# Layer 1's attention in chunks of 1024 keys instead of 512, with PSUM buffers of two banks

## The chip, the cores and the metric

The kernel runs on one core of a Trainium2 chip. A core has five engines with an instruction queue each: TensorE (PE in the profile; its weight loads are listed apart, as PEld), VectorE (DVE), ScalarE (ACT), GpSimd (POOL) and SyncE (SP), which here only issues DMAs. TensorE writes its results into PSUM, 8 banks of 512 fp32 values per partition; DVE and ACT read them there. Everything else lies in SBUF or in DRAM. The metric is the time of one execution on the device in microseconds (us).

## The reference

A trunk of two layers on x of shape 1 x 2048 x 1024, in fp32. Layer 0 (two kinds of windowed attention) is not touched. Layer 1 projects the normalized stream to q, k, v and a gate, and runs differential attention with 8 heads: each head has two score maps over the same keys, and the second is taken off the first with a learned factor. Queries see all keys of their own chunk of 64 and of the chunks before it.

```python
def block(i):                       # 128 queries
    mask = (kchunk[None, :] <= qchunk[:, None])[None, None]
    s1 = jnp.einsum('bqhd,bkhd->bhqk', qb1, k1) * scale
    s2 = jnp.einsum('bqhd,bkhd->bhqk', qb2, k2) * scale
    p1 = jax.nn.softmax(jnp.where(mask, s1, NEG_INF), axis=-1)
    p2 = jax.nn.softmax(jnp.where(mask, s2, NEG_INF), axis=-1)
    a = p1 - lam * p2
    return jnp.einsum('bhqk,bkhd->bqhd', a, v)    # v has 128 columns a head
```

The result of each head goes through an RMS norm, is multiplied with silu(gate), and all heads go through an output projection that is added to the stream.

## The kernel before

Layer 1 runs in two steps: `project` writes q, k, v and the normalized hidden stream to DRAM, and `_mix1` does the rest. The change lies in `_mix1`. There the 2048 queries are 4 blocks of 512 (b = 0 to 3), each of 4 rows of 128 queries (j). A pair of head and block is the unit of work; `heads` runs them as (h, 0), (h, 1) for each of the 8 heads, then block 2 for all heads, then block 3.

**Scores (`scores`, L927 on).** A row with nk visible keys is cut into chunks of up to 512 keys. For each of the two maps (m) and each chunk (z), PE does two matmuls (L949 and L950: the query in a high and a low part, packed against the keys' parts) into one PSUM bank from the pool `pS`, which has `BANKS1[0]` = 4 of them. DVE writes a large negative value over the corner that the last chunk must mask (L952), takes the negated maximum of the chunk (L953), and ACT reads the bank once more and writes exp(score - maximum) into an SBUF tile, with the sum of the row in an accumulator (L956; the read of that accumulator is an ACT record of its own). That exponential is the last reader of the bank. The tiles of the first map come from the pool `pp` (20 tiles of 512), those of the second from `sb` under the tag P1 (8 tiles).

**Joining the chunks (L962 to L976).** Each chunk has its own maximum, so rows of several chunks need factors: the smallest negated maximum, differences, an exponential of them, and sums, on tiny tiles. Rows of one chunk skip this.

**Combining (`combine`, L981 on).** One row later, for each chunk: ACT scales the second map's tile by its factor and lambda (L987), POOL scales the first map's tile (L988) and adds the two (L989). The combined probabilities stay in the first map's tile. `combine` is queued behind the first exponential of the next row.

**Values (`values`).** For each tile of 128 keys, PE transposes the probabilities of up to four rows into a PSUM bank (L1001; pool `ptr`, 2 banks), DVE copies them to SBUF (L1003), and PE multiplies them with v into an accumulator of one bank (L1005; pool `pO`). Then `gate` normalizes and gates the head's output on ACT, DVE and POOL (L1023 to L1037), with one matmul for the mean square (L1033).

**Side work.** `gates` (L1095 on) makes the gate projection, 8 x 8 steps of three matmuls a block (L214 to L216), and `projected` the output projection of finished blocks, in the same form, in the one bank of `pG`; the last block's projection (`projected_last`) runs at the end, when `pS` is free, and keeps its output tiles there.

**Order.** `pace` writes the order: it takes steps of `heads` (each yields a chunk's keys / 256) and of the queue of `values` (each yields its columns / 128) so that the scores lead by `LAG1` (30 or 36) units, and takes side steps in proportion to the units done, by `STAGES1`. This is the order in the code only: the program is built with `schedule_with_timeline_sim=True`, with which the compiler lists the instructions of each engine by a timeline of its own, in the order of the code where operands and buffers are ready. A gate or output step may not come ahead of the score matmul last traced before it (`self.anchor`, `issue_after`). SP issues all loads: q of the next head at row 2, keys and values by `then`, called after each chunk.

## Time and profile before

| | us |
|---|---|
| three runs | 2795.34, 2809.33, 2809.50; median 2809.33 |
| the profiled execution | 2806.47 |
| its span, first to last instruction | 2804.3 |
| first score matmul of layer 1 (L949) starts | 1732.7 |
| last score matmul of layer 1 (L950) starts | 2720.7 |
| 512-key score matmuls of 1 part (L949), in number | 448 |
| score chunks in all (exponentials at L956), in number | 640 |

All rows of the profile come from the one profiled execution; the other runs have a total time only. A row of a group reads: line, engine, operation, written tile <- read tiles, shapes, count | busy time, mean ns of one | idle time of the engine just before them, and what ended it. A row of the waits reads: who waited <- for whom: us in total, times, longest. A row of the timeline reads: start, duration, engine, line, operation. A row of the windows reads: from:to, length, then busy time and number of instructions of each engine, the clock granted to PE as a share of full speed, and DMA. The durations of matmuls are those of a pipelined engine: each overlaps the next, so that their distance from start to start, not their duration, is what they cost.

### The profile page before, as it was taken

Reading aid. Unit: us, or ns where it says so; the run is one execution under the profiler, and the core shown is the slowest. Engines: PE = TensorE matmul, PEld = TensorE weight load, DVE = VectorE, ACT = ScalarE, POOL = GpSimd, SP = SyncE. Lnnn points to the kernel's source line nnn. Section 1 sums busy time; section 2 is a strip of 40 time slices with the busy share of each in tenths; the row PEclk is TensorE's granted clock in tenths of the full one; section 3 lists DMA queues with packets and bytes.
Section 4 is the critical chain, followed back from the end, with each engine's and each line's share of the span. In section 5 each row is a group of like instructions: output and inputs, shape, how many; then the busy total and the mean of one; then the engine's idle time right before and its main releaser. Section 6 shows DMA issues by size and latency. Waiting matters only on the chain.

```text
span 2804.3 us, 43657 instructions
## 1 busy us (share of the span) xinstructions
PE 2691.3 (96%) x13384; PEld 2166.5 (77%) x13384; DVE 1822.1 (65%) x4520; ACT 1599.4 (57%) x3975; POOL 1431.7 (51%) x1519
## 2 busy tenths in 40 slices
PE   7999999999899999999999999999999999999998
PEld 6888887888788888788888888767676777676776
DVE  7752285336777776457834783478886887777762
ACT  5443544357767775333343332578886777776661
POOL 3641254245545454336453652367675666767671
PEclk9999999999999999999999999999999999999999
DMA  5673348739877774754495347788867676464542
GB/s 177 226 240 139 109 148 271 239 111 248 223 196 192 191 196 144 238 190 128 143 297 187 124 134 211 219 232 225 215 194 223 178 210 200 124 190 134 162 154 80
DMA packets 354041, 521.64 MB, mean 186 GB/s; under 512 B 42768, under 2 KB 137744, under 8 KB 353808
## 3 DMA queue, kind: packets, MB, share of 16 engines
q1 hardware_dynamic: 349200, 510.47, 60.6%
q10 hardware_dynamic: 4608, 8.39, 0.8%
q8 instruction: 107, 1.75, 0.3%
q14 instruction: 126, 1.03, 0.1%
HBM read 361.70 MB, written 157.02 MB: 185 GB/s over the span
## 4 chain that ended last, share of the span: by engine, by line
PE 69%; DMA 7%; DVE 3%; ACT 2%; issue 1%; POOL 1%; SPq 0%; ACTq 0%; DVEq 0%; POOLq 0%
PE cO L1005 8%; PE p1mm L216 6%; PE p1mm L215 6%; PE p1mm L214 6%; PE cS L949 4%; PE cS L950 4%; PE ctr L1001 4%; PE com L214 2%; PE com L215 2%; PE com L216 2%; PE mom L214 2%; PE mom L215 2%; PE mom L216 2%; PE mtrB L775 2%; PE cG L214 2%; PE cG L216 2%
## 5 line engine op out<-in xcount | busy, mean ns | idle before, releaser
L956 ACT ACTIVATE cP<-cS,cnm 128x512 f32<-128x512 f32 (+3 forms) x640 | 394.3, 621 | 145.2 <-DVE cnm L953 134.2
L953 DVE TENSOR_REDUCE cnm<-cS 128x1 f32<-128x512 f32 (+3 forms) x640 | 374.7, 602 | 61.5 <-PE cS L950 55.0
L989 POOL TENSOR_TENSOR cP<-cP,cP 128x512 f32<-128x512 f32 (+1 forms) x320 | 358.3, 1148 | 43.7 <-ACT cP L987 43.1
L988 POOL TENSOR_SCALAR cP<-cP,crl,cel 128x512 f32<-128x512 f32 (+3 forms) x288 | 209.9, 743 | 237.9 <-DVE crl L970 136.1
L214 PE MATMUL p1mm<-p1wH,p1hH 128*128 128x512 f32 x768 | 300.1, 392 | 1.2 <-ACT p1hH L334 1.2
L216 PE MATMUL p1mm<-p1wH,p1hL 128*128 128x512 f32 x768 | 300.4, 392 | 0.0
L215 PE MATMUL p1mm<-p1wL,p1hH 128*128 128x512 f32 x768 | 299.3, 390 | 0.0
L309 POOL TENSOR_TENSOR p0wL<-p0ws,p0wH 128x512 fp32r<-128x512 f32 (+1 forms) x140 | 169.9, 1241 | 247.5 <-ACT p0wH L307 228.4
L1005 PE MATMUL cO<-cpt,cv 128*128 128x512 f32 (+3 forms) x640 | 290.1, 538 | 2.9 <-DVE cpt L1003 2.8
L949 PE MATMUL cS<-ck,cqd 128*128 128x512 f32 (+3 forms) x640 | 265.2, 418 | 17.1 <-ACT cP L956 13.7
L1003 DVE COPY cpt<-ctr 128x512 f32<-128x512 f32 (+1 forms) x320 | 191.4, 605 | 112.5 <-PE ctr L1001 109.1
L214 PE MATMUL p0mm<-p0wH,p0hH 128*128 128x512 f32 (+1 forms) x640 | 237.8, 375 | 6.7 <-ACT p0vt L497 4.7
L216 PE MATMUL p0mm<-p0wH,p0hL 128*128 128x512 f32 (+1 forms) x640 | 238.8, 374 | 1.5 <-DVE p0hL L335 1.5
L950 PE MATMUL cS<-ck,cql 128*128 128x512 f32 (+3 forms) x640 | 233.7, 369 | 5.8 <-DMA cql<-qL 5.8
L215 PE MATMUL p0mm<-p0wL,p0hH 128*128 128x512 f32 (+1 forms) x640 | 238.8, 373 | 0.0
L1001 PEld LDWEIGHTS ctr<-ident,cP 128*128 128x128 f32 x1088 | 139.0, 142 | 120.4 <-issue 64.9
L309 POOL TENSOR_TENSOR p1wL<-p1ws,p1wH 128x512 fp32r<-128x512 f32 x112 | 154.4, 1402 | 137.8 <-ACT p1wH L307 126.6
L987 ACT ACTIVATE cP<-cP,cc 128x512 f32<-128x512 f32 (+1 forms) x320 | 189.1, 651 | 22.9 <-DVE cc L973 22.4
L1001 PE MATMUL ctr<-ident,cP 128*128 128x128 f32 x1088 | 177.1, 275 | 5.2 <-ACT csq L1034 3.6
L214 PEld LDWEIGHTS p1mm<-p1wH,p1hH 128*128 128x128 f32 x768 | 144.3, 188 | 29.9 <-ACT p1hH L334 1.4
L216 PEld LDWEIGHTS p1mm<-p1wH,p1hL 128*128 128x128 f32 x768 | 144.2, 188 | 29.4
L215 PEld LDWEIGHTS p1mm<-p1wL,p1hH 128*128 128x128 f32 x768 | 144.3, 188 | 29.1
(302 smaller groups left out, 6945.4 us busy)
## 6 DMA issues: line engine op xcount, KB each, us to landing
p1ws<-in_od_w_in_dram SPq DMA_DIRECT2D x56, 512.0 KB, 3.7
p0ws<-in_ev_w_in_dram SPq DMA_DIRECT2D x48, 512.0 KB, 4.6
ck<-kH SPq DMA_DIRECT2D x144, 128.0 KB, 3.6
ck<-kL SPq DMA_DIRECT2D x144, 128.0 KB, 3.8
cv<-v SPq DMA_DIRECT2D x72, 256.0 KB, 4.3
cqd<-qH SPq DMA_DIRECT2D x64, 256.0 KB, 5.9
cql<-qL SPq DMA_DIRECT2D x64, 256.0 KB, 7.8
cwH<-wgH SPq DMA_DIRECT2D x64, 256.0 KB, 5.4
```

Of the source, the lines that this page charges most:

```text
L214: mm(ps, aH, bH, start=first, stop=False)
L215: mm(ps, aH, bL, start=False, stop=False)
L216: mm(ps, aL, bH, start=False, stop=last)
L309: low.tensor_tensor(l[:, :width], ws[:, k, :width], f32(h[:, :width]), ALU.subtract)
L949: mm(ps, qd[:, m, js], kt[:, :wd], start=True, stop=False)
L950: self.anchor = mm(ps, ql[:, m, js], kt[:, :wd], start=False, stop=True).ins
L953: nc.vector.tensor_reduce(nm[:, m, z:z + 1], ps, AX.X, ALU.max, negate=True)
L956: exp = nc.scalar.activation(chunks[z][:, :wd], ps, AF.Exp, bias=nm[:, m, z:z + 1], accum_out=acc).ins
L988: nc.gpsimd.tensor_scalar(p1, p1, rl[:, 0:1], e1, ALU.mult, ALU.mult)
L989: nc.gpsimd.tensor_tensor(p1, p1, p2, ALU.add)
L1001: nc.tensor.transpose(turned[:, (j - j0) * P:(j - j0 + 1) * P], us[j][kt // 4][:, kk:kk + P], self.ident)
L1005: mm(O[:, j0 * P:], v, T[:, :wd], start=(kt == 0), stop=(kt == nkt - 1), skip_group_check=True)
```

## The change

`WIDE` = 1024. Scores are cut into chunks of up to 1024 keys. The PSUM pool `pS` has 2 buffers of two banks in place of 4 of one; PE fills such a buffer 512 keys at a time, with the same two matmuls for each 512. The mask, the maximum, the exponential, the scaling copy and POOL's two operations then run once for a chunk of up to 1024 keys. Rows of block 1 become one chunk (before: two), those of blocks 2 and 3 two (before: three and four); rows of block 0 stay one chunk of at most 512. The probability tiles become 1024 wide, half as many. In blocks 0 and 2, two chunks of at most 512 keys share such a place (`place_of`). `values` finds its columns by kt // 8 in place of kt // 4. The output projection of the last block takes halves of a two-bank buffer (`bank`), and its weights use three wide P1 places in place of six narrow ones. The number of units that a chunk yields still is its keys / 256, and the lags and stages of `pace` are as before.

```diff
--- before.py
+++ after.py
@@ -24,6 +24,7 @@
 BLK = NTB * P
 NB = S // BLK
 HD = 64
+WIDE = 2 * BLK
 EPS = 1e-6
 NEG = -1e30
 POS = -NEG
@@ -89,7 +90,7 @@
     AHEAD = ((0, 2), (0, 3), (1, 2), (1, 3)), ((0, 5), (1, 0))
     BANKS0, LAG0, SHARE0 = (3, 3, 1, 1), 9, 0.85
     FIN = 18
-    BANKS1, LAG1 = (4, 2, 1, 1), (30, 30, 36, 36)
+    BANKS1, LAG1 = (2, 2, 1, 1), (30, 30, 36, 36)
     STAGES1 = ((0, 0), (44, 84), (1088, 504))
 
     def __init__(self, ctx, tc, args, out):
@@ -895,7 +896,7 @@
         n = "c"
         pool = lambda nm, bufs, **kw: es.enter_context(tc.tile_pool(name=n + nm, bufs=bufs, **kw))
         ld = pool("ld", 2)
-        pp = pool("pp", 20)
+        pp = pool("pp", 10)
         ot = pool("ot", 4)
         vp = pool("v", 4)
         yp = pool("y", 2 * KT)
@@ -929,14 +930,26 @@
 
             qd, ql = q
             us = res["u"] = []
+            halves = [[], []]
+
+            def place_of(m, wd):
+
+                if wd <= BLK and halves[m]:
+                    return halves[m].pop()
+                pl = sb if m else pp
+                t = pl.tile([P, WIDE], F32, tag=f"P{m}", name=n + f"P{m}", bufs=4 if m else None)
+                if wd <= BLK and b % 2 == 0:
+                    halves[m].append(t[:, BLK:])
+                return t
+
             for j in range(NTB):
                 t = b * NTB + j
                 nk = (t + 1) * P
-                cuts = [(c, min(nk, c + 512)) for c in range(0, nk, 512)]
+                cuts = [(c, min(nk, c + WIDE)) for c in range(0, nk, WIDE)]
                 nb = len(cuts)
                 js = slice(j * P, (j + 1) * P)
-                nm = small("nm", 8).rearrange("p (m z) -> p m z", m=2)
-                el = small("el", 16).rearrange("p (m z i) -> p m z i", m=2, i=2)
+                nm = small("nm", 4).rearrange("p (m z) -> p m z", m=2)
+                el = small("el", 8).rearrange("p (m z i) -> p m z i", m=2, i=2)
                 e, la = el[:, :, :, 0], el[:, :, :, 1]
                 l, rl = small("l", 2), small("rl", 2)
                 rows = []
@@ -944,33 +957,36 @@
                     chunks = []
                     for z, (c, ce) in enumerate(cuts):
                         wd = ce - c
-                        ps = pS.tile([P, 512], F32, tag="S", name=n + "S")[:, :wd]
-                        kt = K[z, m]
-                        mm(ps, qd[:, m, js], kt[:, :wd], start=True, stop=False)
-                        self.anchor = mm(ps, ql[:, m, js], kt[:, :wd], start=False, stop=True).ins
+                        ps = pS.tile([P, WIDE], F32, tag="S", name=n + "S")[:, :wd]
+                        for o in range(0, wd, BLK):
+                            oe = min(wd, o + BLK)
+                            kt = K[(c + o) // BLK, m]
+                            mm(ps[:, o:oe], qd[:, m, js], kt[:, :oe - o], start=True, stop=False)
+                            self.anchor = mm(ps[:, o:oe], ql[:, m, js], kt[:, :oe - o], start=False, stop=True).ins
                         if ce == nk:
                             nc.vector.memset(ps[0:HD, wd - 64:], NEG)
                         nc.vector.tensor_reduce(nm[:, m, z:z + 1], ps, AX.X, ALU.max, negate=True)
-                        chunks.append((sb if m else pp).tile([P, 512], F32, tag=f"P{m}", name=n + f"P{m}", bufs=8 if m else None))
+                        chunks.append(place_of(m, wd))
                         acc = la[:, m, z:z + 1] if nb > 1 else l[:, m:m + 1]
                         exp = nc.scalar.activation(chunks[z][:, :wd], ps, AF.Exp, bias=nm[:, m, z:z + 1], accum_out=acc).ins
                         while parts:
                             parts.pop(0)(exp)
-                        then(j, m, z)
+                        for o in range(c, ce, BLK):
+                            then(j, m, o // BLK)
                         yield wd / 256
                     rows.append(chunks)
                 if nb > 1:
-                    top, pe = small("top", 2), small("pe", 8).rearrange("p (m z) -> p m z", m=2)[:, :, :nb]
-                    nc.vector.tensor_reduce(top, nm[:, :, :nb], AX.X, ALU.min)
-                    below = small("below", 8).rearrange("p (m z) -> p m z", m=2)[:, :, :nb]
-                    nc.vector.tensor_tensor(below, nm[:, :, :nb], top.unsqueeze(2).to_broadcast([P, 2, nb]), ALU.subtract)
-                    nc.scalar.activation(e[:, :, :nb], below, AF.Exp, scale=-1.0)
-                    nc.vector.tensor_reduce(pe, el[:, :, :nb, :], AX.X, ALU.mult)
+                    top, pe = small("top", 2), small("pe", 4).rearrange("p (m z) -> p m z", m=2)
+                    nc.vector.tensor_reduce(top, nm, AX.X, ALU.min)
+                    below = small("below", 4).rearrange("p (m z) -> p m z", m=2)
+                    nc.vector.tensor_tensor(below, nm, top.unsqueeze(2).to_broadcast([P, 2, nb]), ALU.subtract)
+                    nc.scalar.activation(e, below, AF.Exp, scale=-1.0)
+                    nc.vector.tensor_reduce(pe, el, AX.X, ALU.mult)
                     nc.vector.tensor_reduce(l, pe, AX.X, ALU.add)
                 nc.vector.reciprocal(rl, l)
-                c2 = small("c2", 4)[:, :nb]
+                c2 = small("c2", 2)[:, :nb]
                 if nb > 1:
-                    nc.vector.tensor_scalar(c2, e[:, 1, :nb], rl[:, 1:2], self.nlam, ALU.mult, ALU.mult)
+                    nc.vector.tensor_scalar(c2, e[:, 1, :], rl[:, 1:2], self.nlam, ALU.mult, ALU.mult)
                 else:
                     nc.vector.tensor_scalar(c2, rl[:, 1:2], self.nlam, None, ALU.mult)
                 parts.append(lambda exp, r=(rows, cuts, e, rl, c2): combine(exp, *r))
@@ -996,9 +1012,9 @@
                 j0 = max(0, kt - b * NTB)
                 wd = (NTB - j0) * P
                 turned = ptr.tile([P, 512], F32, tag="tr", name=n + "tr")
-                kk = (kt % 4) * P
+                kk, ku = (kt % 4) * P, (kt % 8) * P
                 for j in range(j0, NTB):
-                    nc.tensor.transpose(turned[:, (j - j0) * P:(j - j0 + 1) * P], us[j][kt // 4][:, kk:kk + P], self.ident)
+                    nc.tensor.transpose(turned[:, (j - j0) * P:(j - j0 + 1) * P], us[j][kt // 8][:, ku:ku + P], self.ident)
                 T = tp.tile([P, 512], F32, tag="pt", name=n + "pt")
                 nc.vector.tensor_copy(T[:, :wd], turned[:, :wd])
                 v = res["v"][kt // 4][:, kk:kk + P]
@@ -1119,14 +1135,22 @@
                     nc.sync.dma_start(s["g"][c * P:(c + 1) * P, tok], gt)
                     yield 1
 
-        def out_begin(b, j, c, pl=None, tag="S"):
+        banks = []
+
+        def bank(pl):
+
+            if pl is pG:
+                return pG.tile([P, 512], F32, tag="G", name=n + "om")
+            if not banks:
+                t = pS.tile([P, WIDE], F32, tag="S", name=n + "om")
+                banks.extend((t[:, BLK:], t[:, :BLK]))
+            return banks.pop()
+
+        def out_begin(b, j, c, pl=None):
             rows, cols = slice((b * NTB + j) * P, (b * NTB + j + 1) * P), slice(c * 512, (c + 1) * 512)
             xr = ot.tile([P, BLK], F32, tag="ot", name=n + "xr")
             nc.sync.dma_start(xr, self.x1[rows, cols])
-            if b < NB - 1:
-                pl, tag = pG, "G"
-            pl = pl or pS
-            return xr, pl.tile([P, 512], F32, tag=tag, name=n + "om"), self.out[rows, cols]
+            return xr, bank(pG if b < NB - 1 else pl), self.out[rows, cols]
 
         def out_step(b, j, k, ps, w):
             js = slice(j * P, (j + 1) * P)
@@ -1158,16 +1182,11 @@
 
             b = NB - 1
             w = [(room[0][:, k, :], room[1][:, k, :]) for k in range(KT)], []
-            tags = [(ld, "qd"), (ld, "ql")] * 2, [(sb, "P1")] * 6 + [(kp, "k0"), (kp, "k1")]
             pairs = []
-            for pl, tag in tags[0]:
-                t = pl.tile([P, 2, BLK], F32R, tag=tag, name=n + "w" + tag)
+            for pl, tag in [(ld, "qd"), (ld, "ql")] * 2 + [(sb, "P1")] * 3:
+                t = pl.tile([P, 2, BLK], F32R, tag=tag, name=n + "w" + tag, bufs=4 if tag == "P1" else None)
                 pairs.append((t[:, 0, :], t[:, 1, :]))
-            for i in range(4):
-                pairs.append([
-                    pl.tile([P, BLK], F32R, tag=tag, name=n + "w" + tag, bufs=8 if tag == "P1" else None)
-                    for pl, tag in tags[1][2 * i:2 * i + 2]
-                ])
+            pairs.append([kp.tile([P, BLK], F32R, tag=tag, name=n + "w" + tag) for tag in ("k0", "k1")])
             for k in range(KT):
                 load_w(0, k, pairs[k])
             def step(js, tiles, w, k):
@@ -1180,7 +1199,7 @@
             first = [out_begin(b, j, 1) for j in range(NTB)]
             for k in range(KT - 1):
                 yield from step(range(NTB), first, w[0], k)
-            ahead = [out_begin(b, 0, 0, pG, "G")]
+            ahead = [out_begin(b, 0, 0, pG)]
             for k in range(KT - 1):
                 yield from step((0,), ahead, pairs, k)
             yield from step(range(NTB), first, w[0], KT - 1)
```

## The prediction, made before the changed kernel was run

> **What bounds the kernel now.** I read the page first: what each engine does in the whole span, and who is on the chain that ended last.
>
> ```profile
> span 2804.3 us, 43657 instructions
> ...
> PE 2691.3 (96%) x13384; PEld 2166.5 (77%) x13384; DVE 1822.1 (65%) x4520; ACT 1599.4 (57%) x3975; POOL 1431.7 (51%) x1519
> ...
> PE 69%; DMA 7%; DVE 3%; ACT 2%; issue 1%; POOL 1%; SPq 0%; ACTq 0%; DVEq 0%; POOLq 0%
> ```
>
> TensorE (PE) is busy for 96% and has 69% of the chain; no other engine has more than 3%. The change touches only layer 1's attention, so I cut that stretch (it starts near 1733 us and runs to the end) into parts with the view of windows: the start, the interleaved heads of query blocks 0 and 1, block 2, block 3 and the tail. The limits come from the first starts of the score matmuls and the order in `heads`; the inner ones are round numbers that I chose.
>
> ```profile
> core 0: us, PE busy (x) PEld busy (x) DVE busy (x) ACT busy (x) POOL busy (x), PEclk, DMA share, GB/s
> 1733.00:1850.00 117.00, 105.88 (x480) 82.40 (x478) 56.17 (x194) 64.52 (x176) 48.04 (x59) 0.96 0.82 237
> 1850.00:2030.00 180.00, 170.34 (x804) 125.75 (x804) 153.61 (x472) 154.65 (x424) 127.29 (x142) 0.98 0.81 218
> 2030.00:2350.00 320.00, 313.96 (x1434) 230.62 (x1433) 255.08 (x636) 250.78 (x653) 212.96 (x227) 0.99 0.69 204
> 2350.00:2725.00 375.00, 359.23 (x1601) 259.17 (x1600) 276.34 (x623) 266.76 (x684) 259.67 (x264) 0.98 0.50 149
> 2725.00:2804.30 79.30, 70.65 (x299) 52.14 (x296) 18.58 (x29) 11.54 (x19) 16.33 (x15) 0.95 0.32 108
> sum 1071.30, PE 1020.05 PEld 750.08 DVE 759.78 ACT 748.25 POOL 664.30; mean PE 204.01 PEld 150.02 DVE 151.96 ACT 149.65 POOL 132.86
> ```
>
> In 1071 us PE is busy for 1020 and idle for 51. ACT and DVE are nowhere full: they come closest in the second part, at 154.65 and 153.61 of 180 us. So work taken from ACT and DVE is worth only what PE waits for them. That is the view of waits, PE alone, over the same stretch:
>
> ```profile
> PE cS L949 <- ACT cP L956: 13.7, 12, 6.4
> PE cG L214 <- DMA cwH<-wgH: 5.8, 3, 3.3
> PE cS L950 <- DMA cql<-qL: 5.8, 4, 3.3
> PE com L214 <- ACT cyk L1059: 3.7, 1, 3.7
> PE ctr L1001 <- ACT csq L1034: 3.6, 1, 3.6
> PE com L214 <- ACT cy L1059: 3.5, 1, 3.5
> ```
>
> The largest is 13.7 us in 12 waits: a score matmul that waits until an exponential has emptied a PSUM buffer. ACT is named in 13.7 + 3.7 + 3.6 + 3.5 = 24.5 us; the rest is mostly DMA, which the change leaves alone. **24.5 us, 0.9%, is the most that a faster ACT can give.**
>
> **The change part by part.** First the work on ACT and DVE. The view of groups by line, shapes kept apart, has a wide and a narrow form of each operation:
>
> ```profile
> L956 ACT ACTIVATE cP<-cS,cnm 128x512 f32<-128x512 f32 x448 | 305.3, 685 | 121.7 <-DVE cnm L953 112.6 <-PE ctr L1001 3.1 <-DVE cl L969 1.4
> L956 ACT ACTIVATION_READ_ACCUMULATOR cP<-cS,cnm 128x1 f32 x640 | 127.5, 199 | 0.0
> L956 ACT ACTIVATE cP<-cS,cnm 128x128 f32<-128x128 f32 x64 | 23.4, 367 | 10.1 <-DVE cnm L953 8.9 <-DVE cS L952 0.6
> L987 ACT ACTIVATE cP<-cP,cc 128x512 f32<-128x512 f32 x224 | 148.3, 715 | 22.9 <-DVE cc L973 22.4
> L987 ACT ACTIVATE cP<-cP,cc 128x128 f32<-128x128 f32 x32 | 12.6, 394 | 0.0
> ```
>
> ```profile
> L953 DVE TENSOR_REDUCE cnm<-cS 128x1 f32<-128x512 f32 x448 | 300.4, 681 | 58.8 <-PE cS L950 55.0
> L953 DVE TENSOR_REDUCE cnm<-cS 128x1 f32<-128x128 f32 x64 | 17.8, 280 | 0.8
> ```
>
> A line through each pair gives the price of an element and of an instruction. Exponential: (685 - 367) / 384 = 0.83 ns an element, so 685 + 0.83 x 512 = 1109 ns at 1024; two of 512 cost 1370, a merged one saves 261 ns and one accumulator read of 199. Scaling copy: 0.84 ns an element, 1143 ns at 1024, saves 287. Maximum: 1.04 ns an element, 1216 ns at 1024, saves 146. No row has 1024 columns, so these are estimates from the rows above.
>
> How many merge: a row of 128 queries has, per score map, 1, 2, 3 or 4 chunks now (blocks 0 to 3) and 1, 1, 2, 2 after. With 8 heads, 4 rows and 2 maps that is 640 chunks before (the 640 accumulator reads above) and 384 after: 256 merges, and 128 for the copies, which run on one map alone. ACT saves 256 x 0.460 + 128 x 0.287 = 155 us of 748, about 21%. DVE saves 256 x 0.146 = 37 of 760, and in block 1 the five small operations that join two chunks. POOL's two operations also merge; no PE row above waits for POOL, so I cost that at nothing.
>
> PE's own work stays: each piece of 512 keys still takes the same two matmuls, the transposes and value matmuls are the same, and the score units that pace the order sum to 8 x (10 + 26 + 42 + 58) = 1088 in both. For two merged chunks `pace` alternates 4 score units with one value step of 4, where it gave 2 + 2 and then 4; that is nearly the same order.
>
> The relief then is a share of the 24.5 us. Its ends are 0 and -24.5; I take ACT's 21%: **-5 us**. The Trainium skill, "ScalarE: Activation LUTs", section "What ACT_TABLE_LOAD costs", says that back-to-back ACTIVATEs overlap by about 93 ns, which the durations of rows do not show; by it 256 merges would save 24 us less, the relief would be 4 and the sum one higher.
>
> Against this stands **the PSUM**. Four buffers of one bank become two of two banks. A narrow chunk, of at most 512 keys, also takes a whole one. A buffer comes free only after maximum and exponential of the chunk, and the maximum of a wide one starts only when all four matmuls are in. Two places show what that asks. The timeline in a head of block 0:
>
> ```profile
> 1968.02 0.28 PE L950 MATMUL cS<-ck,cql 128*128 128x256 f32 x1
> ...
> 1969.07 0.34 PE L949 MATMUL cS<-ck,cqd 128*128 128x384 f32 x1
> ...
> 1970.88 0.46 ACT L956 ACTIVATE cP<-cS,cnm 128x256 f32<-128x256 f32 x1
> ```
>
> The 256-key chunk whose last matmul starts at 1968.02 is emptied at 1970.88 + 0.46 = 1971.34. The chunk two later (384 keys) starts at 1969.07. With four buffers it may; with two it would come 2.27 us later. Eight such heads: 18 us, if PE did nothing in the gap. In block 2 the wide chunk of one map is followed by that of the other:
>
> ```profile
> 2186.29 0.39 PE L950 MATMUL cS<-ck,cql 128*128 128x512 f32 x1
> ...
> 2195.11 0.47 PE L949 MATMUL cS<-ck,cqd 128*128 128x512 f32 x1
> ...
> 2196.57 0.40 PE L950 MATMUL cS<-ck,cql 128*128 128x512 f32 x1
> ...
> 2197.73 0.40 PE L949 MATMUL cS<-ck,cqd 128*128 128x512 f32 x1
> 2197.97 0.60 PE L1001 MATMUL ctr<-ident,cP 128*128 128x128 f32 x4
> 2198.32 0.48 PE L950 MATMUL cS<-ck,cql 128*128 128x512 f32 x1
> ```
>
> Filled by about 2196.9, emptied 1.22 + 1.11 us later at the earliest, 2199.2: the other map's chunk, at 2197.73, would be 1.5 us late. The chunk before it, filled at 2186.7, had until 2195.11 and would cost nothing. If half of block 2's 32 rows are of the tight kind: 16 x 1.5 = 24 us.
>
> Do these gaps stand idle? The last three rows say that PE's order is not that of the code: four transposes stand between the two matmuls of one chunk, which the code writes one behind the other. The compiler's list had moved other ready work in. So the bounds are 0 and 18, 0 and 24. I take a third of each, as PE has transposes, value and gate matmuls to move, but the list can't fill what it doesn't foresee: **+6 and +8 us**. Blocks 1 and 3 have wide chunks with longer distances; I take nothing there, which is the weakest zero.
>
> The other edits I cost at nothing. Probability places: 20 of 512 become 10 of 1024, and 8 become 4 for the second map, the same storage. Counted along `pace`'s order, each place is freed by transposes that stand ahead of the scores that need it; the smallest distance falls from 13 steps of that order to 1, in row 2 of block 2's heads, so PE has passed it; were it late, the exponential would hold ACT's queue (the scaling copies behind it, and POOL's additions behind those) for one value step. In the tail the output tiles take halves of two buffers: the third waits for two additions in place of one, behind seven other matmul groups. No DMA is added, and SP's order stays: `then` still runs for each 512 keys, up to one chunk later.
>
> **Sum.** The profiled execution took 2806.5 us (span 2804.3 and 2.2 around it); 2806.5 - 5 + 6 + 8 = 2815.5. The median of the runs shown, 2809.3, lies 3 above it, so the forecast is 2815, within 0.5% of both; 0.5%, 14 us, is about what a measurement of this kernel can tell from no change.
>
> **Rivals.** A, slower: two buffers in place of four, and the list does not fill the gaps. For it speaks that the largest engine wait is already of this kind (13.7 us), that its first place is where ACT and DVE are fullest, and that the distances fall below what the rows show as needed. Price: the full 18 + 24 less the relief of 5 gives 2843; with three quarters of it, 2833. It decides from the point at which a buffer's emptying (3 us in block 0) exceeds the spacing of two chunks and no ready work is queued. The Trainium skill, "Perfetto Trace Analysis", section "Matmuls", has independent groups rotate through different banks so that the evacuation of one overlaps the next group; by that rule fewer, larger steps of rotation cost time, which is this rival. No run here has shown it yet.
>
> B, faster: the gaps are filled completely, and the lighter ACT removes two thirds of the 24.5 us: 2806.5 - 16 = 2790; all of it would be 2782. For it speaks that PE stays busy through 314 of 320 us in block 2 although ACT takes 251; against it, that single waits of 3.5 us and more at L1059 and L1034 follow a head's end, where a shorter exponential changes little.
>
> **How the numbers follow.** Forecast 0.47, A 0.35, B 0.18. The range 2788 to 2850 reaches into both rivals: B's last third and the part of A where blocks 1 and 3 stall too are left out. The forecast's own range is 2800 to 2823. Faster by over 0.5% is B, slower is A, the rest is the forecast.
>
> **What would show it.** Right: ACT's busy time in this stretch near 590 us, maxima near 1.2 us, PE's matmul counts unchanged, waits of L949's successor on the exponential between 12 and 28 us, mostly in block 0 and block 2. Rival A: those waits above 35 us. Rival B: those below 8 us. I would be wrong if wide instructions cost more an element than narrow ones, or if the new order puts DMA waits where none were.

## The result and the profile after

| | before | after |
|---|---|---|
| runs, median | 4 runs, 2804.79 us | 4 runs, 2874.24 us |
| lowest to highest | 2795.34 to 2809.50 | 2870.20 to 2877.48 |
| ratio of times | 1 | 1.0256, interval 1.0228 to 1.0284 |
| span of the profiled execution | 2804.3 | 2875.6 |

The changed kernel is 2.6% slower: 69 us. The forecast was 2815 with a range up to 2850, so even the range was too low. From the page of the changed kernel, the rows that answer to those shown of before:

```profile
span 2875.6 us, 42085 instructions
...
PE 2716.4 (94%) x13384; PEld 2169.6 (75%) x13384; DVE 1792.4 (62%) x4136; ACT 1516.6 (53%) x3303; POOL 1361.3 (47%) x1263
...
PE 64%; DMA 7%; DVE 5%; ACT 4%; issue 2%; POOL 1%; SPq 1%; DVEq 0%; ACTq 0%; POOLq 0%
```

PE runs the same 13384 matmuls, ACT, DVE and POOL run 672, 384 and 256 instructions fewer, and the span is 71.3 us longer. On the chain of work that ended last, PE lost five points and ACT and DVE won four: the softmax engines now stand where they hardly stood before.

To see where in the attention the time went, both traces are cut at the same events: ACT's copies (L1023 before, L1039 after) that take the 16th, the 24th and the 32nd head's output. So the first stretch holds blocks 0 and 1, the second block 2, the third block 3, the fourth the tail. The view of windows, before:

```profile
1733.00:2065.00 332.00, 311.22 (x1447) 234.63 (x1446) 240.68 (x747) 251.06 (x684) 201.62 (x227) 0.97 0.79 220
2065.00:2360.30 295.30, 289.26 (x1316) 211.87 (x1315) 231.64 (x572) 225.21 (x590) 192.06 (x205) 0.99 0.70 204
2360.30:2772.30 412.00, 396.14 (x1761) 285.35 (x1759) 280.81 (x624) 268.86 (x679) 268.08 (x271) 0.98 0.49 145
2772.30:2804.30 32.00, 23.43 (x89) 18.23 (x89) 6.65 (x10) 3.13 (x5) 2.54 (x2) 0.88 0.31 107
```

and after:

```profile
1735.00:2094.40 359.40, 325.95 (x1442) 242.81 (x1441) 216.18 (x542) 226.67 (x473) 179.12 (x159) 0.95 0.72 201
2094.40:2409.00 314.60, 293.29 (x1312) 210.09 (x1310) 230.33 (x500) 203.10 (x413) 173.87 (x136) 0.99 0.66 192
2409.00:2843.10 434.10, 404.08 (x1770) 285.02 (x1768) 274.07 (x517) 231.91 (x395) 238.34 (x151) 0.99 0.46 139
2843.10:2875.60 32.50, 23.48 (x89) 18.28 (x89) 6.69 (x10) 3.12 (x5) 2.54 (x2) 0.88 0.30 105
sum 1140.60, PE 1046.81 PEld 756.21 DVE 727.27 ACT 664.80 POOL 593.86; mean PE 261.70 PEld 189.05 DVE 181.82 ACT 166.20 POOL 148.46
```

Lengths compared: **+27.4 us in blocks 0 and 1, +19.3 in block 2, +22.1 in block 3**, +0.5 in the tail. With a start that is 2 us later that is the whole 71.3. (The scores of a head run ahead of its output, so each stretch ends with the first scores of the next block.) PE's idle time (length less busy) rose from 51 to 94 us, and its busy time by 27.

The matmuls being the same, the trace shows two sources of those 27 us. The durations of all PE rows of the first three stretches sum to 8 us more: in the first stretch the clock is granted at 0.95 in place of 0.97, and the trace's record of it has 37.5 us at half speed there, for 17.1 before (worth about 10 us, an estimate). And the part of these durations that lies beside another matmul's is 19 us less: PE stands idle 106 times in place of 40, and a matmul that follows an idle time overlaps nothing before it.

What PE waits for in the changed kernel, from the first score matmul on:

```profile
PE cS L964 <- ACT cP L971: 58.9, 56, 6.0
PE cO L1021 <- DVE cpt L1019: 5.4, 10, 1.2
PE ctr L1017 <- POOL cP L1005: 4.1, 4, 1.2
```

The first row is the one that was 13.7 us in 12 waits: a score matmul held until an exponential has emptied a PSUM buffer. It is now 58.9 us in 56 waits, and no other row is above 5.4. By stretch it is 24.7, 15.8 and 18.4 us, where before had 8.1, 1.9 and 3.7. The row names the engine that ended the wait, not its cause: an exponential that is late for a reason of its own holds its score buffer as well. The timeline shows one such wait, in a head of block 0 whose chunks stand among the wide ones of block 1:

```profile
1951.16 0.47 PE L964 MATMUL cS<-ck,cqd 128*128 128x512 f32 x1
...
1953.31 1.23 DVE L968 TENSOR_REDUCE cnm<-cS 128x1 f32<-128x1024 f32 x1
...
1953.67 0.33 PE L964 MATMUL cS<-ck,cqd 128*128 128x128 f32 x1 [0.43 <-ACT cP L971]
...
1955.58 1.10 ACT L971 ACTIVATE cP<-cS,cnm 128x1024 f32<-128x1024 f32 x1
...
1956.82 0.47 PE L964 MATMUL cS<-ck,cqd 128*128 128x128 f32 x1 [2.71 <-ACT cP L971]
```

The wide chunk, begun at 1951.16, holds one two-bank buffer until its exponential ends at 1956.68. A 128-key chunk takes the other at 1953.67. The next 128-key chunk finds none and stands 2.71 us, though the chunk ahead of it fills a quarter of one of its two banks. Part of that is ACT's queue: the wide chunk's maximum was ready at 1954.54, and its exponential began 1.04 us later, behind a scaling copy and a step of the gate. Of the 15 waits of the first stretch, 11 with 18.7 of the 24.7 us are at chunks of 384 keys or fewer, all of them block 0's. One of the 11, with 5.99 us, stands behind a late load (last section). Two waits, 2.3 us, are those of block 2's first scores.

In block 2 the waits are short and regular, 19 of at most 1.8 us. The timeline there:

```profile
2298.03 0.22 PE L964 MATMUL cS<-ck,cqd 128*128 128x128 f32 x1
...
2298.10 1.11 ACT L971 ACTIVATE cP<-cS,cnm 128x1024 f32<-128x1024 f32 x1 [0.74 <-DVE cnm L968]
...
2299.36 0.50 PE L964 MATMUL cS<-ck,cqd 128*128 128x512 f32 x1 [1.00 <-ACT cP L971]
...
2303.16 0.50 PE L964 MATMUL cS<-ck,cqd 128*128 128x512 f32 x1 [1.06 <-ACT cP L971]
```

A row of block 2 is 1024 keys and a narrow rest. The rest (128 keys here, begun at 2298.03) takes a whole buffer and gives PE a quarter of a microsecond of work, while the wide chunk's buffer is emptied until 2299.21; the second map's wide chunk waits for that. The same follows 3.8 us later for the next.

The merged instructions themselves have the durations that were estimated (groups, shapes kept apart):

```profile
L971 ACT ACTIVATE cP<-cS,cnm 128x1024 f32<-128x1024 f32 x160 | 178.1, 1113 | 117.6 <-DVE cnm L968 93.9 <-PE ctr L1017 12.5 <-DVE crl L986 7.3
L968 DVE TENSOR_REDUCE cnm<-cS 128x1 f32<-128x1024 f32 x160 | 195.3, 1222 | 44.7 <-PE cS L965 42.7
```

1113 and 1222 ns stand against 1109 and 1216. In the first row there is a second thing: ACT's exponential waited 12.5 us for transposes (PE L1017). An exponential waits for a transpose when the SBUF place that it writes to is still being read. Over all widths that is 12.9 us in 7 waits; before, it was 3.2 us in 7.

So there are two suspects: **two score buffers in place of four**, and **probability places of 1024**, which come free in larger portions. A third is the order: `pace` takes steps of up to 4 units where it took 2. A fourth is the length of ACT's bursts, as a scaling copy of 1.14 us can stand ahead of an exponential on ACT's queue.

### The profile page after: what moved, and what is told of

It is laid out like the page before. It is cut to its first block, busy times and chain, and to the rows that moved or that the text cites. A ratio compares the mean times of both kernels' runs of the same rounds, so it can differ in the third digit from the quotient of the medians.

```text
span 2875.6 us, 42085 instructions
## 1 busy us (share of the span) xinstructions
PE 2716.4 (94%) x13384; PEld 2169.6 (75%) x13384; DVE 1792.4 (62%) x4136; ACT 1516.6 (53%) x3303; POOL 1361.3 (47%) x1263
## 3 DMA queue, kind: packets, MB, share of 16 engines
q1 hardware_dynamic: 349200, 510.47, 58.9%
## 4 chain that ended last, share of the span: by engine, by line
PE 64%; DMA 7%; DVE 5%; ACT 4%; issue 2%; POOL 1%; SPq 1%; DVEq 0%; ACTq 0%; POOLq 0%
PE cO L1021 8%; PE p1mm L217 6%; PE p1mm L215 6%; PE p1mm L216 6%; PE cS L964 4%; PE cS L965 3%; PE ctr L1017 3%; PE mom L215 2%; PE mom L216 2%; PE mom L217 2%; PE com L215 2%; PE com L217 2%; PE com L216 2%; PE mtrB L776 2%; ACT cP L971 2%
## 5 line engine op out<-in xcount | busy, mean ns | idle before, releaser
L971 ACT ACTIVATE cP<-cS,cnm 128x1024 f32<-128x1024 f32 (+7 forms) x384 | 330.8, 863 | 244.5 <-DVE cnm L968 209.1
L1005 POOL TENSOR_TENSOR cP<-cP,cP 128x1024 f32<-128x1024 f32 (+2 forms) x192 | 333.2, 1750 | 159.3 <-ACT cP L1003 159.0
L968 DVE TENSOR_REDUCE cnm<-cS 128x1 f32<-128x1024 f32 (+7 forms) x384 | 348.3, 911 | 50.9 <-PE cS L965 42.7
L964 PE MATMUL cS<-ck,cqd 128*128 128x512 f32 (+3 forms) x640 | 267.2, 419 | 62.2 <-ACT cP L971 58.9
L1017 PEld LDWEIGHTS ctr<-ident,cP 128*128 128x128 f32 x1088 | 138.9, 142 | 123.7 <-issue 68.7
L1004 POOL TENSOR_SCALAR cP<-cP,crl,cel 128x1024 f32<-128x1024 f32 (+7 forms) x128 | 130.1, 1027 | 167.3 <-DVE crl L986 111.7
L964 PEld LDWEIGHTS cS<-ck,cqd 128*128 128x128 f32 x640 | 123.3, 193 | 112.4 <-ACT cP L971 87.5
L1017 PE MATMUL ctr<-ident,cP 128*128 128x128 f32 x1088 | 178.4, 276 | 6.6 <-POOL cP L1005 4.1
L1003 ACT ACTIVATE cP<-cP,cc 128x1024 f32<-128x1024 f32 (+2 forms) x192 | 165.1, 892 | 21.7 <-DVE cc L989 20.2
```

Source lines behind the costliest of these rows:

```text
L964: mm(ps[:, o:oe], qd[:, m, js], kt[:, :oe - o], start=True, stop=False)
L968: nc.vector.tensor_reduce(nm[:, m, z:z + 1], ps, AX.X, ALU.max, negate=True)
L971: exp = nc.scalar.activation(chunks[z][:, :wd], ps, AF.Exp, bias=nm[:, m, z:z + 1], accum_out=acc).ins
L1005: nc.gpsimd.tensor_tensor(p1, p1, p2, ALU.add)
L1017: nc.tensor.transpose(turned[:, (j - j0) * P:(j - j0 + 1) * P], us[j][kt // 8][:, ku:ku + P], self.ident)
```

## The experiments

Every time below is a median. Each ratio, with its 95% interval, is to runs of the kernel before that were made beside it on the same chip; their medians lie between 2801.83 and 2805.19 us. The stretches are from one profiled execution each, cut as above. A wait row is from the first score matmul to the end, unless a stretch is named.

| kernel | median us | ratio (interval) | 16th head out at | block 2 | block 3 |
|---|---|---|---|---|---|
| before | 2804.79 | 1 | 2065.0 | 295.3 | 412.0 |
| after | 2874.24 | 1.0256 (1.0228 to 1.0284) | 2094.4 | 314.6 | 434.1 |
| e1_places | 2847.61 | 1.0154 (1.0133 to 1.0175) | 2067.3 | 295.6 | 448.8 |
| e2_two | 2988.04 | 1.0648 (1.0627 to 1.0668) | 2114.9 | 338.9 | 501.5 |
| e4_ring | 3320.75 | 1.1844 (1.1822 to 1.1867) | 2237.2 | 450.2 | 596.4 |
| e9_ring512 | 3687.52 | 1.3144 (1.3120 to 1.3169) | 2325.9 | 517.5 | 795.7 |
| e5_places_fine | 2834.27 | 1.0112 (1.0084 to 1.0140) | 2057.0 | 293.0 | 443.0 |
| e6_grain | 2813.39 | 1.0045 (1.0025 to 1.0064) | 2069.7 | 290.9 | 414.7 |
| e7_halfstep | 2894.56 | 1.0332 (1.0302 to 1.0361) | 2104.8 | 330.2 | 428.5 |
| e8_spread | 2870.20 | 1.0244 (1.0219 to 1.0269) | 2093.3 | 311.7 | 432.4 |
| e9b_first_map | 2801.71 | 0.9996 (0.9984 to 1.0007) | 2068.9 | 291.9 | 407.9 |
| e9c_second_map | 2837.69 | 1.0118 (1.0103 to 1.0134) | 2068.3 | 296.9 | 437.9 |
| e10_after_places | 2865.12 | 1.0212 (1.0191 to 1.0233) | 2100.2 | 319.2 | 414.4 |
| e11_wide_in_3 | 2801.05 | 0.9982 (0.9970 to 0.9994) | 2065.8 | 296.9 | 403.2 |
| e12_wide_from_2 | 2824.17 | 1.0079 (1.0061 to 1.0097) | 2070.5 | 316.8 | 403.5 |
| e13_three | 2853.35 | 1.0184 (1.0166 to 1.0202) | 2075.2 | 303.1 | 439.4 |
| e14_two_pools | 2822.63 | 1.0071 (1.0046 to 1.0096) | 2074.0 | 298.9 | 416.4 |
| e15_block0_two | 2860.40 | 1.0210 (1.0191 to 1.0228) | 2117.2 | 294.3 | 416.1 |
| e16_apart_narrow | 2830.68 | 1.0094 (1.0073 to 1.0114) | 2099.0 | 301.8 | 402.8 |
| e17_apart_wide_1 | 2854.35 | 1.0184 (1.0169 to 1.0199) | 2098.1 | 319.0 | 405.4 |

### Fewer score buffers alone

The kernel before with two, and with three, score buffers of one bank; the banks left over serve only the output tiles of the tail.

```diff
-    BANKS1, LAG1 = (4, 2, 1, 1), (30, 30, 36, 36)
+    BANKS1, LAG1 = (2, 2, 1, 1), (30, 30, 36, 36)     # e13_three: (3, 2, 1, 1)
+        pX = pool("pX", 4 - NS, space=PSUM)
```

> The kernel before with two PSUM score buffers of one bank in place of four (the other two banks are kept for the tail's output tiles alone). No wide instruction, no wide place. Theory 1: the waits on the exponential rise from 13.7 us to above 60, and the time to 2860 or more. Rivals 2 and 3 (places, or long instructions): at most 2820.

> The kernel before with three PSUM score buffers of one bank in place of four (two gave 2988). If time follows the number of chunks in flight: 2830 to 2880. If three are enough for the distance at which exponentials follow: 2802 to 2815.

The waits on the exponential, in e2_two:

```profile
PE cS L951 <- ACT cP L958: 116.8, 134, 8.6
```

and in e13_three:

```profile
PE cS L951 <- ACT cP L958: 38.6, 37, 3.2
```

So the kernel before has no buffer to spare: the fourth is worth 1.8%, the third another 4.6. The loss falls in all stretches, in block 3 most (+27 and +90 us). The wait row accounts for part of it only: 103 us of 184 with two buffers, 25 of 51 with three. Most of the rest is PE's busy time, which rises as in the changed kernel, by 76 and 16 us in the three stretches, with a clock granted at 0.96, 0.97 and 0.95 where two buffers are left.

### Four banks as one ring: not what it was meant to be

The changed kernel with the four banks as slices of one PSUM tile, given out in turn, so that a narrow chunk takes one bank and a wide one two; and the same ring with chunks of 512.

```diff
-        pS = pool("pS", NS, space=PSUM)
+        pS = pool("pS", 1, space=PSUM)
+        ring, at_bank = pS.tile([P, 4, BLK], F32, tag="S", name=n + "S"), [0]
...
-                        ps = pS.tile([P, WIDE], F32, tag="S", name=n + "S")[:, :wd]
+                        ps = banks_of(wd)
```

> The changed kernel with its four score banks handed out one by one in a ring: a wide chunk takes two neighbouring banks, a chunk of at most 512 keys one. Block 0 then has four chunks in flight again; blocks 1 and 3 are as in the changed kernel, and block 2's wide chunks still use the same pair. Theory 1 with my place for it (narrow chunks that hold a whole two-bank buffer): the stretch to the end of blocks 0 and 1 gets 10 to 20 us shorter, the time is 2852 to 2864. If the narrow chunks don't matter: 2870 to 2878.

> The ring of four banks with chunks of 512 everywhere, and places of 1024 that two chunks share; the order's steps are those of the kernel before. A control for the ring and for the shared places. Theory 1: as before, 2805 us within 14. If handing out banks in a fixed turn costs by itself: above 2820.

Both are far slower than any theory had it. The timeline of e9_ring512 says why:

```profile
2902.27 0.69 DVE L979 TENSOR_REDUCE cnm<-cS 128x1 f32<-128x512 f32 x1 [2.25 <-PE cS L976]
...
2903.00 0.69 ACT L982 ACTIVATE cP<-cS,cnm 128x512 f32<-128x512 f32 x1 [2.11 <-DVE cnm L979]
...
2903.83 0.80 PE L975 MATMUL cS<-ck,cqd 128*128 128x512 f32 x1 [0.38 <-ACT cP L982]
...
2905.16 0.69 DVE L979 TENSOR_REDUCE cnm<-cS 128x1 f32<-128x512 f32 x1 [2.19 <-PE cS L976]
```

Matmul, maximum, exponential, and only then the next chunk's matmul, though that goes to another bank: one chunk is in flight at a time. In this program slices of one tile are waited for as one buffer. So these runs say nothing about a true ring. They do carry the count of buffers down to one (with places of 1024, which cost 1.1% of their own, below), and with e2_two and e13_three give a series of time over before: four buffers 0, three +51 us, two +184, one +884 (chunks of 512). For chunks of 1024: two (the changed kernel) +69, one +517. (A part of the rings' loss is the clock, granted at 0.88 and 0.93 on the mean for 0.99 before.) At equal count the wide chunk is the better one; the change loses because it halves the count.

### Probability places alone

Chunks of 512 and four score buffers, as before; only the places are 1024 wide (10 and 4 for 20 and 8), two chunks to a place. In e1_places `scores` also yields once for two chunks, as in the changed kernel; in e5_places_fine once a chunk, as before. e6_grain is the kernel before with those coarse steps and nothing else.

```diff
-        pp = pool("pp", 20)
+        pp = pool("pp", 10)
...
-                        chunks.append((sb if m else pp).tile([P, 512], F32, tag=f"P{m}", name=n + f"P{m}", bufs=8 if m else None))
+                        chunks.append(place_of(m, wd))
...
-                        yield wd / 256                  # e1_places and e6_grain alone
+                        owed += wd / 256
+                        if z % 2 or z == nb - 1:
+                            yield owed
+                            owed = 0
```

> Only the SBUF half of the change: places of 1024, half as many and freed by eight key tiles, and the coarser steps of the order (a step is yielded for two chunks together). Scores, maxima, exponentials and combination stay at 512 with four PSUM buffers of one bank. Theory 1 (the loss is two PSUM buffers in place of four): as before, 2805 us within 14, waits of the score matmul on the exponential under 20 us. Rival 2 (places freed later and the coarser order): most of the 70 us, at or above 2840. Rival 3 (long instructions on ACT and DVE): as before, since all are short here.

> The first run moved places and order together and took 43 us. This has the wide places alone: scores, exponentials and steps as before. If the places are the cause (a place is freed after eight key tiles, so the exponentials of block 3 get theirs later): 2835 to 2850. If the coarser steps are: 2805 within 14.

> The kernel before with the coarser steps alone: a step of the order is given for two chunks of 512 together, all buffers and places as before. If the steps are the cause: 2835 to 2850. If the places are: 2805 within 14.

The places alone cost 1.1%, the coarse steps alone 0.45%. All of the places' loss is in block 3 (443.0 for 412.0); the other stretches are as before or shorter. (The profiled execution, at 2826.44 us, is the shortest of its four.) With both edits, e1_places passes the first stretch and block 2 as before does, 2067.3 and 295.6: **with four score buffers, neither places nor steps cost anything there.** The next pair asks which map's places: 14 in place of 10 for the first, or 7 in place of 4 for the second.

```diff
-        pp = pool("pp", 10)
+        pp = pool("pp", 14)               # e9b_first_map
...
-                t = pl.tile([P, WIDE], F32, tag=f"P{m}", name=n + f"P{m}", bufs=4 if m else None)
+                t = pl.tile([P, WIDE], F32, tag=f"P{m}", name=n + f"P{m}", bufs=7 if m else None)      # e9c_second_map
```

> The wide places alone (scores of 512, fine steps; 2834 us with 10 and 4 places), now with 14 places for the first map. If block 3's exponentials wait for places of the first map, which are held until the transposes of eight key tiles: back to 2802 within 14. If it is the second map's, or the width itself: 2825 to 2840.

> The same with 10 places for the first map and 7 for the second (before: 4). If the second map's places, held until POOL has added both chunks in them, are the cause: back to 2802 within 14. If the first map's are: 2825 to 2840.

Block 3 in the view of windows, first in e5_places_fine:

```profile
2350.00:2793.00 443.00, 406.87 (x1769) 287.17 (x1767) 293.90 (x631) 270.23 (x684) 265.15 (x271) 0.98 0.47 136
```

then in e9b_first_map:

```profile
2360.80:2768.70 407.90, 392.94 (x1762) 284.75 (x1760) 282.01 (x624) 268.38 (x678) 265.65 (x271) 0.99 0.50 147
```

PE idles 36 us in the first and 15 in the second; before it was 16. What PE waits for in block 3, first in e5_places_fine, then in e9b_first_map:

```profile
PE cS L965 <- ACT cP L972: 15.4, 13, 2.3
```

```profile
PE cS L965 <- ACT cP L972: 2.7, 3, 1.5
```

Both have four score buffers of one bank, as before (3.7 us). An exponential that finds no place keeps its score buffer, and PE waits for that: the row that looks like a lack of score buffers is raised by places alone. So the changed kernel's 18.4 us in block 3 can't be put down to its two buffers alone. ACT's waits for a place, in e5_places_fine, from the first score matmul on:

```profile
ACT cP L972 <- PE ctr L1018: 19.2, 10, 3.1
```

With 14 places that row is gone from the view; with seven places for the second map it stays (9.0 us in block 3, for 10.1 with four and 3.1 before). So it is the first map's places. The code says why: transposes go through the key tiles in order, all rows of the head for each. After four key tiles the first 512 keys of all four rows are read, and four places of 512 are free; places of 1024 are free only after eight. A head of block 3 holds 8 places of 10, so the next head gets two ahead and then stands. (That is read from the code; what the runs show is that 14 places remove it.)

More places in the changed kernel itself:

```diff
-        pp = pool("pp", 10)
+        pp = pool("pp", 12)
...
-                t = pl.tile([P, WIDE], F32, tag=f"P{m}", name=n + f"P{m}", bufs=4 if m else None)
+                t = pl.tile([P, WIDE], F32, tag=f"P{m}", name=n + f"P{m}", bufs=6 if m else None)
```

> The changed kernel with 12 and 6 places in place of 10 and 4; nothing else. If the places cost it in block 3 what they cost alone (22 to 31 us): 2843 to 2858, with the stretches of blocks 0 to 2 still some 48 us longer than before. If two PSUM buffers are all of its loss: 2868 to 2880.

Block 3 falls from 434.1 to 414.4, within 3 us of before, and its waits for score buffers from 18.4 to 11.4 us. The kernel as a whole gains 9 us only, which lies between the two expectations: the 16th head is out 6 us later and block 2 takes 5 us more, and no run says why. What is left of the loss, 33 and 24 us, is ahead of block 3, with this row over the whole:

```profile
PE cS L964 <- ACT cP L971: 59.3, 51, 5.5
```

The sum is that of the changed kernel, but its parts have moved: 31.5, 16.4 and 11.4 us by stretch, for 24.7, 15.8 and 18.4. So places are the cause of most of block 3's loss, and of none of the others'. Which map's places did it here is not separated. ACT's own waits for a place in block 3 did not fall (15.3 us for 8.9), so how 20 us came back is shown by the pair above and not in this kernel.

### The order and the bursts

In the changed kernel, e7_halfstep yields after each 512 keys of a wide chunk; e8_spread puts one scaling copy behind each exponential in place of two.

```diff
+                            if oe < wd:                    # e7_halfstep
+                                yield BLK / 256
...
-                        while parts:                       # e8_spread
+                        if parts:
                             parts.pop(0)(exp)
```

> The changed kernel, with a wide chunk's two halves as two steps of the order, so that value and side steps can stand between its first and second pair of matmuls, as they stand between two chunks before. If the coarser steps cost it something: 2830 to 2862. If two wide buffers and the places are all of it: 2868 to 2880, or worse, since a buffer is held longer while it fills.

> The changed kernel with one scaling copy behind each exponential of the next row in place of both behind the first, so that ACT is held for 1.1 us at a time and not for 2.1. If long bursts on ACT, which delay the exponential that frees a buffer, are a good part of the loss (rival 3): 2840 to 2862. If not: 2866 to 2880.

e8_spread is the changed kernel's time again (2870.20 for 2874.24): bursts of two copies on ACT, which only blocks 2 and 3 have, are not the cause. Rows of blocks 0 and 1 have one copy in both kernels, so the run says nothing of the first stretch. e7_halfstep is slower still. In it the first value steps of a head stand ahead of the combination of its last row and read the uncombined map (as its code has it), so its dependencies differ, and it doesn't settle what the coarse steps cost in the changed kernel. For the kernel before, e6_grain has the answer: 0.45%, of which nothing is in block 2 (290.9).

### Wide chunks in some blocks only

Four one-bank buffers up to a block, then that pool is closed and opened again as two two-bank buffers; chunks of 512 before that point and of 1024 from there on; 14 places for the first map. e11_wide_in_3 changes over at block 3, e12_wide_from_2 at block 2.

```diff
+CUT = (512, 512, 512, 1024)               # e12_wide_from_2: (512, 512, 1024, 1024)
...
-                        ps = pS.tile([P, WIDE], F32, tag="S", name=n + "S")[:, :wd]
+                        ps = sc[0].tile([P, CUT[b]], F32, tag="S", name=n + "S")[:, :wd]
...
+                if b == 3 and len(sc) == 1:
+                    narrow.close()
+                    sc.append(0)
+                    sc[0] = pool("pW", NS // 2, space=PSUM)
```

> Four PSUM buffers of one bank and chunks of 512 in blocks 0 to 2; from block 3 on two buffers of two banks and chunks of 1024; 14 and 4 places. If the two buffers lose only where chunks are narrow or of mixed width (blocks 0 to 2, 48 us in the changed kernel): those stretches are as before, and the time is 2795 to 2820. If two wide buffers cost block 3 as much as the others (20 us each): 2820 to 2840.

> As the kernel with wide chunks in block 3 alone (2801 us), but wide from block 2 on, with two buffers of two banks there; 14 and 4 places. If block 2's wide chunks, with a narrow one between them, are what loses its 19 us: 2815 to 2828, in block 2's stretch alone. If they aren't: 2790 to 2810.

Blocks 2 and 3 in e11_wide_in_3:

```profile
2065.80:2362.70 296.90, 291.23 (x1325) 213.14 (x1323) 229.04 (x561) 223.24 (x561) 191.75 (x200) 0.99 0.71 205
2362.70:2765.90 403.20, 390.99 (x1750) 284.42 (x1750) 269.03 (x508) 225.91 (x387) 236.51 (x149) 0.99 0.50 147
```

and in e12_wide_from_2:

```profile
2070.50:2387.30 316.80, 296.66 (x1333) 212.94 (x1331) 237.32 (x509) 208.49 (x424) 180.67 (x142) 1.00 0.67 193
2387.30:2790.80 403.50, 390.72 (x1751) 283.52 (x1750) 269.49 (x508) 225.46 (x386) 234.19 (x148) 0.99 0.50 146
```

**Block 3 with wide chunks on two buffers isn't slower** than with narrow ones on four: 403 us, against 408 with the same 14 places (e9b_first_map) and 412 before. PE idles 12 us there. **Block 2 is slower by 20**: PE idles 20 us in place of 6, and is busy 5 us more for about the same matmuls. Its waits on the exponential rise from 0.7 us to 17.0 in 21 waits of at most 1.7. The two blocks differ in what stands beside the wide chunk: a row of block 3 is 1024 keys and 640 to 1024 more; one of block 2 is 1024 and 128 to 512 more, so half of its chunks put at most 512 keys into a two-bank buffer.

e11_wide_in_3 is 0.2% under the kernel before. Its interval excludes 1, but single runs of the kernel before, made beside it, lie up to 0.6% apart (2795.89 to 2812.52 us).

### Blocks 0 and 1

Two pairs of kernels ask which of the two blocks loses the first stretch's 27 us. In the first pair, four one-bank buffers are split in two groups that take turns (e14_two_pools, the control); then block 0 uses one group alone (e15_block0_two).

```diff
+        def from_pool(alone=False):
+            turn[0] += 1
+            return pS if alone or turn[0] % 4 in (1, 2) else pX
...
-                        ps = pS.tile([P, 512], F32, tag="S", name=n + "S")[:, :wd]
+                        ps = from_pool().tile([P, 512], F32, tag="S", name=n + "S")[:, :wd]      # e15_block0_two: from_pool(b == 0)
```

> Control: the kernel before with its four score buffers in two groups of two, given in a fixed turn (two chunks from the one, two from the other). 2802 within 14 if the fixed turn costs nothing.

> As the control, but the chunks of block 0 take the first group alone, so that they have two buffers as in the changed kernel; all other blocks have four. If block 0's narrow chunks are what loses the 27 us of the first stretch: 15 to 30 us above the control, in that stretch. If they aren't (wide chunks of block 1, or both): under 8.

The fixed turn itself costs 0.7%. Block 0 on two buffers costs 38 us beyond it, above both expectations and in the first stretch, but by another way, as its PE waits there say:

```profile
PE cS L955 <- DMA cqd<-qH: 24.4, 6, 9.5
PE cS L955 <- ACT cP L962: 8.4, 10, 3.9
```

In the control the two are 6.3 and 5.8 us. What is late is the load of q, which the changed kernel doesn't show at all among its first rows, and the waits on the exponential rise by 2.6 us only. So this run can't stand for the changed kernel.

In the second pair all heads of block 0 run first, then all of block 1 (e16_apart_narrow, with block 3 wide as in e11_wide_in_3); then wide chunks from block 1 on (e17_apart_wide_1).

```diff
-            order = [(h, b) for h in range(8) for b in range(2)] + [(h, b) for b in range(2, NB) for h in range(8)]
+            order = [(h, b) for b in range(NB) for h in range(8)]
...
-CUT = (512, 512, 512, 1024)
+CUT = (512, 1024, 1024, 1024)             # e17_apart_wide_1
-                if b == 3 and len(sc) == 1:
+                if b == 1 and len(sc) == 1:
```

> As the kernel with wide chunks in block 3 alone, but all heads of block 0 run first, then all of block 1: the control for the next. The order differs and keys are loaded again for block 1, so the time may be anywhere from 2790 to 2850.

> The same order, wide chunks and two buffers from block 1 on; block 0 has four buffers of one bank. If block 1's wide chunks cost nothing on two buffers, and the first stretch is lost by block 0's narrow chunks: 15 to 26 us above the control, all in block 2. If block 1's wide chunks lose it: 35 to 55 above.

Blocks 1 and 2, narrow, in e16_apart_narrow:

```profile
1912.40:2099.00 186.60, 179.97 (x831) 131.85 (x830) 157.09 (x451) 154.29 (x416) 128.86 (x140) 0.99 0.82 220
2099.00:2400.80 301.80, 289.57 (x1310) 210.88 (x1308) 226.25 (x557) 220.54 (x552) 186.94 (x195) 0.98 0.69 200
```

and wide, in e17_apart_wide_1:

```profile
1908.60:2098.10 189.50, 180.60 (x812) 131.32 (x812) 133.57 (x274) 128.48 (x229) 103.21 (x74) 0.97 0.76 210
2098.10:2417.10 319.00, 297.48 (x1329) 213.42 (x1327) 236.61 (x508) 207.85 (x422) 179.46 (x140) 0.99 0.68 194
```

Block 1 by itself loses 2.9 us by wide chunks on two buffers: its rows are one chunk of 640 to 1024 keys. Block 2 loses 17.2 again. So blocks whose chunks are all over 512 lose next to nothing, and the block that mixes loses its 17 to 20 us each time (24 in e10_after_places). The first stretch's 27 us are then left to the narrow chunks of block 0 on two buffers, among the wide ones of block 1: places and steps cost nothing there with four buffers (e1_places), block 1's wide chunks by themselves next to nothing, and the wait rows of the changed kernel point there as well (18.7 of 24.7 us at chunks of 384 keys or fewer). That is found by exclusion; no run isolates it, since in these two kernels block 0 keeps its four buffers.

## Why the prediction was wrong, by its own steps

**The durations and PE's work: right.** 1113 and 1222 ns at 1024 columns, PE's 13384 matmuls unchanged.

**ACT's 155 us: the durations right, what they are worth half as much.** The three groups (exponentials, accumulator reads, copies) sum to 710.9 us before and 570.5 after, 140 less. ACT's busy time in the windows fell only from 748 to 665 us, and "near 590" was wrong. The page of the Trainium skill that the prediction kept out of its sum has the difference: "ScalarE: Activation LUTs", section "What ACT_TABLE_LOAD costs", lets back-to-back ACTIVATEs overlap by about 93 ns. The trace agrees, for the accumulator reads too:

```profile
1955.58 1.10 ACT L971 ACTIVATE cP<-cS,cnm 128x1024 f32<-128x1024 f32 x1
1956.57 0.19 ACT L971 ACTIVATION_READ_ACCUMULATOR cP<-cS,cnm 128x1 f32 x1
1956.66 0.36 ACT L971 ACTIVATE cP<-cS,cnm 128x128 f32<-128x128 f32 x1
```

Each begins about 0.1 us ahead of the end of the one before it. Of 640 instructions that went, 0.1 us each was never ACT's time: 64 us (an estimate).

**The relief of 5 us: not seen as such in the changed kernel, small where it could be.** The row it was to come from rose from 13.7 to 58.9 us. In block 3 of e11_wide_in_3, where two buffers don't bite, ACT is busy 42 us less than in e9b_first_map, and the stretch is 4.7 us shorter, which is of the order of the prediction's 5 but within what two executions of one kernel differ by.

**The PSUM: mechanism right, size wrong; this is the first step that failed.** The bounds were 18 us for block 0 and 24 for block 2, and of each a third was taken, on the view that the compiler's list would fill the gaps. It fills few: the first stretch lost 27 us, above its bound, and block 2 lost 19 (17 to 20 when tried apart), four fifths of its bound. In block 2 the mechanism is the one foreseen, the second map's wide chunk held by the first map's: 1.5 us late at 16 of the rows was the bound, 19 waits of up to 1.8 us, 0.8 on the mean, were measured. The upper bound for block 0 was too low because it counted the wait alone, one a head. Waits on the exponential rose by 16.6 us in that stretch, within the bound, while those on DMAs fell from 11.6 to 3.7, so that PE idles 12.7 us more; what the bound left out is the rise of PE's busy time by 14.7 us, the clock behind a stall (about 10, the estimate above) and overlap lost.

**The zero for blocks 1 and 3: right for their score buffers** when each was tried with 14 places and, for block 1, apart from block 0: 2.9 us and none.

**The places at nothing: wrong; the second step that failed.** It was found by counting along `pace`'s order, where each place is freed ahead of its use. But the prediction itself had shown that the list which the engines run is not that order. It had also seen the smallest distance fall from 13 steps to 1, and called 1 enough; it saw that in block 2, and the loss is in block 3. For a late place it foresaw ACT's queue held for one value step, and left out that the score buffer is held with it. Measured alone the places cost 1.1%, 31 us in block 3, and 14 places in place of 10 take all of it back. In the changed kernel block 3 loses 22, of which two more places for each map take back 20.

**Rival A was the right mechanism** ("the list does not fill the gaps") for the stretches ahead of block 3. Its sign, waits above 35 us, came true as 58.9, or 40.5 without block 3, whose waits places raise as well. Its price of 2833 to 2843 holds only the score buffers. With block 3's 22 us its upper end would be 2865. The 2874 measured come with three more terms: the first stretch lost 9 more than its bound, block 2 lost 5 less, and the relief of 5 isn't seen. The rule that the prediction named beside it (the Trainium skill, "Perfetto Trace Analysis", section "Matmuls": independent groups rotate through different banks, so that one's evacuation overlaps the next) agrees with e13_three and e2_two, and needs a closer word for this kernel: what counts is how many chunks can be held and released independently. The rings of four banks rotated through different banks and were slowest.

What stays open: whether the 27 us of the first stretch come from block 0's two buffers alone or need the interleaving with wide chunks; how much of them is ACT's queue, which held the exponential in the wait shown above; and whether the coarse steps, 0.45% in the kernel before, cost the changed kernel anything.

## What to carry to other kernels

On an engine that is busy for 96%, count how many independently released buffers stand ahead of it, and check each size of work: a small piece in a large buffer holds all of it. Merging two instructions on an engine that isn't the bound is worth at most what the bound waits for that engine (here 24.5 us, 13.7 of them at score buffers), and costs as soon as a buffer count or a release comes in larger portions; storage that is equal in bytes isn't equal in time. A row of waits says who came last and not why: here the same row rose by fewer score buffers and by places alone. Where the list of instructions differs from the code's order, a distance of one step along the code's order is no cover.
